# Rotary embedding and attention scores: all batch loads on SyncE's ring, and three groups of tiny loads behind stores

## The chip, the cores and the metric

The kernel runs on one core of one Trainium2 chip. The metric is the device time of that core in microseconds (us); lower is better. Engines: TensorE (PE), VectorE (DVE), ScalarE (ACT), GpSimd (POOL) and SyncE (SP), and 16 DMA engines that all queues of the core share.

## What is computed

Rotary embedding of q and k, then the scores of every query with every key, per batch and head. All is float32; batch 16, sequence 512, 16 heads of 64.

```python
q1, q2 = q[..., :half_dim], q[..., half_dim:]
q_rot = np.concatenate([q1 * cos_q - q2 * sin_q, q1 * sin_q + q2 * cos_q], axis=-1)
# k_rot from k in the same way
scores = np.einsum('bshd,bthd->bsht', q_rot, k_rot)
```

q and k are 33.6 MB each, the output is 268.4 MB.

## The kernel before, in words

The work goes in 64 steps `i`, four per batch. A step makes one output tile `st` of 128 query rows x 16 heads x 512 keys, 4 MB, and stores it with one DMA (`store`, L192). In the first batch (steps 0 to 3) the tile is stored in four quarters of 1 MB instead (L215).

Loads: q and k of a batch (2 MB each) come as one tile of 128 rows x 16 KB into `in_pool`, which has two buffers for each of q and k. Row p holds the sequence positions 4p to 4p+3. Batch 0 comes in smaller pieces (`early`) at the start. In the main loop, after step `i`, the q load of batch `i // 4 + 2` is asked for if `i % 4 == 2`, and the k load of batch `i // 4 + 3` if `i % 4 == 3`.

Compute of a step: DVE rotates the next rows of q and k (`rope`, three full-size operations each: L153, L154, L158). TensorE transposes them by a product with an identity (L174) into PSUM, from where DVE or ACT copies them into `qT` or `kT` (L189). Then `scores` makes 8 head pairs per step: two products of 64 x 128 by 64 x 512 (L205) into a PSUM tile of two banks, and one ACT copy of 128 x 1024 into `st` (L212). `stage_pool` has three buffers for `st`: ACT's first copy of step `i` has to wait until the store of step `i - 3` has landed.

What sets the order: the program is written out by hand (`tc.manual_schedule()`), so every engine issues in the order of the code. SyncE issues nearly all DMAs: the store of a step, then a load if that step asks for one, then the store of the next step. A DMA of 128 rows is cut into 8 rows for each of the 16 DMA engines. For SyncE and ACT together, the DMAs take 8 completion semaphores ("lanes") in turn, and each DMA waits for the one that had its lane before, the eighth ahead of it.

Five of the loads are made otherwise in before: those that stand in `RELIEVED` (q of batches 6, 11 and 15, k of batches 7 and 12) are made by `load_around` (L89 to L115). There GpSimd loads rows 0 to 119 as a DMA of 120 rows, which takes 15 of the DMA engines with 8 rows each. `move_cursor` issues tiny GpSimd loads into `scratch` ahead of it, which move the place at which GpSimd's next DMA starts, so that one chosen engine (`SLOW = 4`) is the one left out. The last 8 rows are loaded by a second DMA, cut into pieces of 2 KB: on ACT's queue for q, on GpSimd's for k. The issue is on POOL or ACT, so these loads do not stand in SyncE's order.

Of the kernel before, what the change touches and what calls it, by code (L numbers as in the profile page):

```python
# [10 lines left out]
def kernel(  # L11
# [8 lines left out]
    nc = tc.nc  # L20
# [53 lines left out]
    batches = {}  # L74

    RELIEVED = {("q", 6): 0, ("k", 7): 1, ("q", 11): 2, ("k", 12): 3, ("q", 15): 4}
    SLOW = 4
    scratch = const_pool.tile([P, 96], fp32, name="scratch")
    tiny = [0]  # L80

    def move_cursor(n):

        y = tiny[0]
        tiny[0] += 1
        src = bass.AP(q.tensor, 512 * y, [(512, n), (64, 2), (1, 2)])
        nc.gpsimd.dma_start(scratch[:n, 4 * y : 4 * y + 4].rearrange("p (a b) -> p a b", a=2), src)

    def load_around(which, b, t):  # L89

        n, E, SMALL = 120, C * H * D, C * H * D // 8
        x = RELIEVED[which, b]
        d = dram[which][b]

        def pieces(queue, lo, hi, F):
            k = E // F
            src = bass.AP(d.tensor, d.offset + lo * E + E - F, [(E, hi - lo), (-F, k), (1, F)])
            v = t[lo:hi].rearrange("p c e -> p (c e)")  # L100
            dst = bass.AP(v.tensor, v.offset + E - F, [v.ap[0], (-F, k), (1, F)])
            queue.dma_start(dst, src)  # L102

        if x == 0:
            nc.gpsimd.inc_swdge_sem([], [], mode="reset_dge_cursor")
        else:

            move_cursor(16 - SLOW)
        if x % 2:
            move_cursor(8)  # L110
            pieces(nc.gpsimd, n, P, SMALL)
        move_cursor(SLOW + 1)
        pieces(nc.gpsimd, 0, n, E // 2)
        if not x % 2:
            pieces(nc.scalar, n, P, SMALL)  # L115

    def load(which, b):
# [4 lines left out]
        batches[which, b] = t  # L122
        if (which, b) in RELIEVED:
            load_around(which, b, t)
# [66 lines left out]
    def store(i, st):  # L191
        nc.sync.dma_start(o_v[i // C, i % C], st)  # L192

    def scores(i, p, st):

        ps = ps_s_pool.tile([P, 2, S], fp32, tag="ps_s", name="ps")
        b = i // C
        if b == 0:
            c, hp = divmod(p, 2)
            lhs, rhs = qT[i][:, C * hp + c], kT[0][:, 2 * i + hp]  # L200
        else:
            lhs, rhs = qT[i][:, p], kT[b][:, p]
        for r in range(2):
            po, rh = ps[:, r, :], rhs[64 * r : 64 * r + 64, :]
            nc.tensor.matmul(  # L205
                out=po, lhsT=lhs[64 * r : 64 * r + 64, :], rhs=rh, start=True, stop=True
            )
        so, si = st[:, 2 * p : 2 * p + 2, :], ps
        if b > 0:
            so = so.rearrange("s r (t c) -> s r t c", c=C)  # L210
            si = si.rearrange("s r (c t) -> s r t c", c=C)
        nc.scalar.copy(out=so, in_=si)  # L212
        if b == 0 and p % 2 == 1:
            c = p // 2
            nc.sync.dma_start(o_v[0, c, :, G * i : G * (i + 1)], st[:, G * c : G * (c + 1)])  # L215
        elif b > 0 and p == HP - 1:
            store(i, st)

    def tr_act(which, n):
        for g in range(2):  # L220
            transposed(which, n, g, nc.scalar.copy)
# [5 lines left out]
    with tc.manual_schedule():  # L227
# [16 lines left out]
        for i in range(C):  # L244
            st = st_first[i] if i < 2 else stage_pool.tile([P, H, S], fp32, tag="stage", name="st")
            if i < C - 1:
                dve = rope("k", i + 1) + rope("q", i + 1) + rope("k", C + i)
                nxt = [("k", i + 1), ("q", i + 1)]
            else:
                dve = rope("q", C) + rope("k", C + i) + rope("q", C + 1) + rope("k", 2 * C)  # L250
                nxt = [("q", C), ("k", C + i)]
            for p in range(HP):
                scores(i, p, st)
                if p in (0, 1) and i > 0:
                    run(dve[:1])
                    dve = dve[1:]
                    transposed("k", C + i - 1, p, nc.vector.tensor_copy)
                if p == 3 and i < 2:
                    load("kq"[i], 2)
                if p in (2, 6):  # L260
                    m = len(dve) - (4 if p == 2 else 2) - (2 if i == C - 1 else 0)
                    run(dve[:m])
                    dve = dve[m:]
                    tr_act(*nxt.pop(0))
            run(dve)
# [3 lines left out]
        for i in range(C, NST):  # L269
            tr = {}  # L270
            if i + 1 < NST:
                tr[1], tr[3] = ("q", i + 1, 0), ("q", i + 1, 1)
            if i + C < NST:
                tr[5], tr[6] = ("k", i + C, 0), ("k", i + C, 1)
            dve = []
            if i + 2 < NST:
                dve += rope("q", i + 2)
            if i + 1 + C < NST:
                dve += rope("k", i + 1 + C)
            st = stage_pool.tile([P, H, S], fp32, tag="stage", name="st")  # L280
            for p in range(HP):
                scores(i, p, st)
                if p not in tr:
                    continue
                if tr[p][0] == "q":
                    run(dve[:1])
                    dve = dve[1:]
                    transposed(*tr[p], nc.vector.tensor_copy)
                else:
                    transposed(*tr[p], nc.scalar.copy)  # L290
            run(dve)
            if i % C == C - 2:
                load("q", i // C + 2)
            elif i % C == C - 1:
                load("k", i // C + 3)
# [30 lines left out]
```

## Time and profile before

| what | value |
|---|---|
| time, median of 2 runs | 793.2 us (792.83 to 793.57) |
| span of the profiled execution, first to last instruction | 789.9 us |
| busy: PE / ACT / DVE / POOL | 687.7 / 561.2 / 543.8 / 11.9 us |
| HBM read / written | 67.24 / 268.44 MB, 425 GB/s over the span |
| stores of 4 MB, issue to landing, median | 25.2 us |
| SyncE waiting for ACT to fill a 4 MB tile (60 stores) | 663.3 us in total |
| GpSimd's loads of 1920 KB, issue to landing, median | 29.2 us (q), 43.2 us (k) |

The span is that of one execution under the profiler; the median of the runs lies 3.3 us above it. How to read the lines that follow: "DMA" in the 40 slices is the mean busy share of the 16 DMA engines in tenths. q1 is SyncE's queue, q0 GpSimd's, q10 ACT's. In the chain of work that ended last, a line gives the start, the length and what was waited for: "DMA out_dram<-st" is the time from the issue of a store to its landing. In a timeline, the first column is the start in us from the beginning of the span, the second how long the issuing instruction (or, with xN, a run of N of them) took, and "SPq" is SyncE as the issuer.

### The profile page before, as it was taken

The page shows a single profiled execution, that of the slowest core. Times are in us where ns is not written, and L with a number is a line of the kernel's source. Part 1 is how long each engine was busy: PE and PEld are TensorE (multiplying, and loading weights), DVE is VectorE, ACT ScalarE, POOL GpSimd, SP SyncE. Part 2 cuts the span into 40 slices and gives each one's busy share as a digit, 9 for nine tenths or more (in the row PEclk, how much of TensorE's full clock was granted, in tenths as well). Part 3 has the DMA queues.
Part 4 walks back from the last instruction along what each step waited for, and adds up shares of the span by engine and source line. Part 5 has one row for each costly group of instructions (what it writes and reads, how often), then busy time and mean ns, then how long its engine had stood idle before and what let it go on. Part 6 is the DMA issues. An engine that isn't in the chain of part 4 may idle for free.

```text
span 789.9 us, 7753 instructions
## 1 busy us (share of the span) xinstructions
PE 687.7 (87%) x3072; PEld 297.4 (38%) x3072; DVE 543.8 (69%) x516; ACT 561.2 (71%) x647; POOL 11.9 (2%) x24
## 2 busy tenths in 40 slices
PE   4999998989978989798897988989899798899960
PEld 2444443433423434243343433434334343344420
DVE  7999987667855859566676666767678486587400
ACT  3888886866847868486685865877577586588770
POOL 0000000000001000000000000100000000000000
PEclk9999999999998999899899898999899899899995
DMA  9999999999999999999999999999999999999997
GB/s 353 421 426 440 429 431 435 424 434 440 428 427 429 429 425 406 428 431 436 430 431 434 427 431 427 429 432 429 427 437 422 437 433 433 428 431 436 430 431 339
DMA packets 19100, 336.18 MB, mean 426 GB/s; under 512 B 2376, under 2 KB 3656, under 8 KB 4936
## 3 DMA queue, kind: packets, MB, share of 16 engines
q1 hardware_dynamic: 16288, 324.61, 96.1%
q0 software_dynamic: 1872, 10.10, 3.1%
q10 hardware_dynamic: 904, 0.98, 0.4%
q8 instruction: 24, 0.39, 0.2%
q14 instruction: 12, 0.10, 0.0%
HBM read 67.24 MB, written 268.44 MB: 425 GB/s over the span
## 4 chain that ended last, share of the span: by engine, by line
DMA 46%; PE 39%; DVE 7%; ACT 4%; issue 1%; ACTq 0%
DMA out_dram<-st 45%; PE ps L205 29%; PE bank L174 9%; ACT st L212 4%; DVE part L153 2%; DVE early L154 1%; DVE early L158 1%; DMA early<-in_q_dram 1%; DVE k_sb L158 1%; DVE k_sb L154 1%; DVE kT_t L189 0%; DVE q_sb L154 0%; DVE q_sb L158 0%; ACTq L321 0%; DVE qT_t L189 0%
## 5 line engine op out<-in xcount | busy, mean ns | idle before, releaser
L212 ACT COPY st<-ps 128x1024 f32<-128x1024 f32 x512 | 495.0, 1020 | 193.7 <-DMA out_dram<-st 109.1
L205 PE MATMUL ps<-kT_t,qT_t 64*128 64x512 f32 x2048 | 545.6, 650 | 64.3 <-ACT st L212 64.1
L205 PEld LDWEIGHTS ps<-kT_t,qT_t 64*128 64x128 f32 x2048 | 183.3, 196 | 255.3 <-issue 135.4
L189 DVE COPY qT_t<-bank 128x512 f32<-128x512 f32 x118 | 81.5, 690 | 186.5 <-PE bank L174 186.5
L174 PEld LDWEIGHTS bank<-ident,q_sb 128*128 128x128 f32 x480 | 55.4, 151 | 100.5 <-issue 97.6
L174 PE MATMUL bank<-ident,q_sb 128*128 128x128 f32 x480 | 86.8, 308 | 0.4 <-PE ps L205 0.4
L174 PEld LDWEIGHTS bank<-ident,k_sb 128*128 128x128 f32 x480 | 50.3, 140 | 94.6 <-issue 42.3
L174 PE MATMUL bank<-ident,k_sb 128*128 128x128 f32 x480 | 78.6, 287 | 1.2 <-DVE qT_t L189 1.2
L153 DVE TENSOR_TENSOR part<-k_sb,ss_t 128x1024 f32<-128x1024 f32 x60 | 72.9, 1215 | 9.3 <-DMA k_sb<-in_k_dram 9.2
L189 ACT COPY kT_t<-bank 128x512 f32<-128x512 f32 x122 | 72.4, 598 | 6.9 <-PE bank L174 6.9
L154 DVE TENSOR_TENSOR k_sb<-k_sb,cos_t 128x1024 f32<-128x1024 f32 x60 | 73.5, 1225 | 2.0
L158 DVE TENSOR_TENSOR k_sb<-k_sb,part 128x1024 f32<-128x1024 f32 x60 | 73.5, 1225 | 2.1
L154 DVE TENSOR_TENSOR q_sb<-q_sb,cos_t 128x1024 f32<-128x1024 f32 x60 | 73.5, 1225 | 2.1
L153 DVE TENSOR_TENSOR part<-q_sb,ss_t 128x1024 f32<-128x1024 f32 x60 | 73.5, 1224 | 2.0
L158 DVE TENSOR_TENSOR q_sb<-q_sb,part 128x1024 f32<-128x1024 f32 x60 | 72.9, 1215 | 0.0
L174 PE MATMUL bank<-ident,early 128*128 128x128 f32 x64 | 10.5, 316 | 12.2 <-DVE early L158 9.7
L174 PEld LDWEIGHTS bank<-ident,early 128*128 128x128 f32 x64 | 8.3, 161 | 17.3 <-issue 13.9
L153 DVE TENSOR_TENSOR part<-early,ss_t 128x1024 f32<-128x1024 f32 x8 | 9.8, 1222 | 5.7 <-DMA early<-in_k_dram 4.9
L102 POOL DMA_DIRECT2D q_sb<-in_q_dram x3 | 2.3, 754 | 617.4 <-PE bank L174 617.4
L158 DVE TENSOR_TENSOR early<-early,part 128x512 f32<-128x512 f32 x16 | 10.3, 685 | 0.2
L154 DVE TENSOR_TENSOR early<-early,cos_t 128x1024 f32<-128x1024 f32 x8 | 9.8, 1225 | 0.3
L189 ACT COPY qT_t<-bank 128x512 f32<-128x512 f32 x10 | 5.7, 628 | 3.3 <-PE bank L174 3.3
(12 smaller groups left out, 15.9 us busy)
## 6 DMA issues: line engine op xcount, KB each, us to landing
out_dram<-st SPq DMA_DIRECT2D x60, 4096.0 KB, 25.2
k_sb<-in_k_dram SPq DMA_DIRECT2D x13, 2048.0 KB, 27.7
q_sb<-in_q_dram SPq DMA_DIRECT2D x12, 2048.0 KB, 27.6
out_dram<-st SPq DMA_DIRECT2D x16, 1024.0 KB, 14.5
q_sb<-in_q_dram POOLq DMA_DIRECT2D x3, 1920.0 KB, 29.2
k_sb<-in_k_dram POOLq DMA_DIRECT2D x2, 1920.0 KB, 43.2
early<-in_k_dram SPq DMA_DIRECT2D x1, 1536.0 KB
early<-in_q_dram SPq DMA_DIRECT2D x1, 1536.0 KB, 12.4
```

Source lines behind the costliest of these rows:

```text
L102: queue.dma_start(dst, src)
L153: nc.vector.tensor_tensor(pv, xs, ss, op=mult)
L154: nc.vector.tensor_tensor(xc, xc, cs, op=mult)
L158: nc.vector.tensor_tensor(y, y, z, op=add)
L174: nc.tensor.transpose(bank[:, x, :], src, ident)
L189: copy(out=dst, in_=src)
L205: nc.tensor.matmul(out=po, lhsT=lhs[64 * r : 64 * r + 64, :], rhs=rh, start=True, stop=True)
L212: nc.scalar.copy(out=so, in_=si)
```

## The change

`RELIEVED` is emptied, so `load_around` and `move_cursor` are called no more and all 30 batch loads after batch 0 are made by SyncE (L126 before, L132 after). A new function `marks` issues 15 tiny loads on SyncE, of n = 1 to 15 rows of three float32 each, into columns of `scratch` that nothing reads. It is called right behind the store of steps 10, 34 and 60, so ahead of the q load that steps 10 and 34 ask for.

```diff
-    RELIEVED = {("q", 6): 0, ("k", 7): 1, ("q", 11): 2, ("k", 12): 3, ("q", 15): 4}
+    RELIEVED = {}
...
+    def marks():
+
+        for n in range(1, 16):
+            src = bass.AP(q.tensor, 512 * n, [(4096, n), (1, 3)])
+            nc.sync.dma_start(scratch[:n, 45 + 3 * n : 48 + 3 * n], src)
...
         elif b > 0 and p == HP - 1:
             store(i, st)
+            if i in (10, 34, 60):
+                marks()
```

In the compiled order this takes 19 rows from POOL and six from ACT's list, and adds 50 to SyncE's: 45 tiny loads and the 5 batch loads. The orders of TensorE and DVE stay as they were.

## Prediction

> **What bounds the kernel now.** I read the page first, then the chain that ended last, then SyncE's issues, then the trace's records of single packets and landings. From the page:
>
> ```profile
> span 789.9 us, 7753 instructions
> ...
> DMA  9999999999999999999999999999999999999997
> GB/s 353 421 426 440 429 431 435 424 434 440 428 427 429 429 425 406 428 431 436 430 431 434 427 431 427 429 432 429 427 437 422 437 433 433 428 431 436 430 431 339
> ...
> q1 hardware_dynamic: 16288, 324.61, 96.1%
> q0 software_dynamic: 1872, 10.10, 3.1%
> ```
>
> The 16 DMA engines are busy from the first slice to the last; the two queues alone make 99.2%. No engine of the core stands at that share all along. So the end is set by the slowest of the 16 engines, and what counts is how much that one has to do and how long it stands idle. The chain's longest pieces show its pace:
>
> ```profile
> 113.28 25.54 DMA out_dram<-st
> 159.42 28.77 DMA out_dram<-st
> 207.39 30.89 DMA out_dram<-st
> 260.35 24.02 DMA out_dram<-st
> 305.15 30.61 DMA out_dram<-st
> 356.54 28.25 DMA out_dram<-st
> 406.99 27.18 DMA out_dram<-st
> 455.57 28.16 DMA out_dram<-st
> 505.95 23.87 DMA out_dram<-st
> 550.84 29.48 DMA out_dram<-st
> 599.51 29.51 DMA out_dram<-st
> 649.81 29.32 DMA out_dram<-st
> 739.70 20.22 DMA out_dram<-st
> ```
>
> Start plus length is when a store has landed in full, on its last engine: steps 8, 12, 16, ... 52, then 60. Landings are 138.82, 188.19, 238.28, 284.37, 335.76, 384.79, 434.17, 483.73, 529.82, 580.32, 629.02, 679.13, 759.92. Four steps move four stores and two loads, 20.97 MB. In the packet records a 32 KB packet takes 1.21 us on every engine, a store so 9.7 us, a load 4.85, and four steps would be 48.5. The differences are 49.37, 50.09, **46.09**, 51.39, 49.03, 49.38, 49.56, **46.09**, 50.50, 48.70, 50.11. The two short ones are where GpSimd issued two loads each around one engine (from 227.75 and 472.79). All others are longer than 48.5: one engine is late. The packet records name no engine, but each packet starts 3 to 4 ns before the end of the one ahead of it, so chains can be followed: on one engine packets take 10 to 50 ns over the 1213, some 1 us in every 50 and 15.5 us in all; the other fifteen have exactly 1213, but for some lumps.
>
> The last thing to see is what SyncE does behind store 10, which it issued at 133.44 (the last of the x3):
>
> ```profile
> 113.28 20.50 SPq L192 DMA_DIRECT2D out_dram<-st  x3
> 133.87 0.56 SPq L126 DMA_DIRECT2D q_sb<-in_q_dram  x1
> 149.40 0.33 SPq L192 DMA_DIRECT2D out_dram<-st  x1
> ```
>
> By its landing events store 10 lands between 154.98 (first engine) and 158.64 (last). The load behind it and store 11 stand in the rings long before: that is why the engines never run dry.
>
> **Part 1: the loads go back to SyncE's ring.** Removed: on POOL 5 big loads, 2 of 8 rows and 11 tiny ones, on ACT 3 loads of 8 rows. POOL does nothing else, and ACT gets back under 3 us of issue (3 x 0.7 to 1.3) while it waits for DMA anyway (109.1 us of idle before the copies of L212): no gain. SyncE issues 5 loads more, 5 x 0.5 us, in stretches in which it waits for ACT (663.3 us in its waits): no cost. The bytes are the same. What goes is the relief. I extend the chain without it. Seven of the unrelieved differences (all but the two right after a relief, 51.39 and 50.50, in which all engines had long packets) have a mean of 49.46. Eleven of these from 138.82 end at 682.9, against 679.13. Steps 53 to 60 hold 8 stores and one load, 82.45 us, at that pace 84.1: 767.0, against 759.92. The three last stores and the rest took 30.0, at that pace 30.6: 797.6. So the relief's loss is **+7.7 us**. Ends: with 49.03, the difference farthest from any POOL load, the same sum gives +2.0; with the mean of all nine unrelieved, 49.79, it gives +12.0. I take 7.7, since another count comes near it: an engine with no drip and no extra rows would end near 780.5, plus 15.5 of drip is 796.
>
> **Part 2: the marks.** In the compiled order every DMA of SyncE waits for the semaphore lane of the DMA eight places ahead of it; there are 8 lanes. Before, that one had always landed. Now 15 marks stand behind store 10 (and 34, and 60). Marks 1 to 7 wait for older transfers and at latest for store 9; mark 8 has the lane of the store itself and waits for it **to land**. SyncE issues in order, so marks 9 to 15, the load of q (steps 10 and 34) and the next store, long filled, are all held behind mark 8. When the store's last engine ends, nothing is left in any ring. From then on, per group:
> - last packet to landing to wake: 0.4 us (the last packet of the kernel ends 788.62, landed 789.02);
> - marks 8 to 15 issued, 8 x 0.49 us. Small loads at the start are the nearest rows:
>
> ```profile
> 0.74 0.43 SPq L70 DMA_DIRECT2D early<-in_k_dram  x1
> 1.23 0.45 SPq L230 DMA_DIRECT2D cos_t<-in_cos_dram  x1
> ```
>
>   0.74 to 1.23, and the next one at 1.74: 0.49 and 0.51 apart, so 3.9 us. Marks 9 to 15 wait for marks 1 to 7, which sit right behind the store and land with it. The next big DMA waits for mark 8 too, but a small first load landed 2.9 us after its issue (sin_t), which is within the 3.9;
> - its issue to its first packet: 1.1 us (0.74 to the first data packet at 1.82).
>
> Sum 5.4 us in which the late engine is idle, and the others longer. Nothing covers it: no other ring holds work now. It is not won back, since the engines are the bound. PE and ACT do not prolong it: they fill the other two stage buffers meanwhile, so that two stores follow at once. Three groups: **+16.2 us**. The transferred bytes (1.4 KB a group) are nothing. Ends: a spacing of 0.43 (133.44 to 133.87) gives 4.9 a group, and 4.6 with a faster start, 13.8 in all; the spacing of ACT's loads of 8 rows, 0.73 at least and 0.78 with a gap, gives 7.7, 23 in all. Nearest are SyncE's own small loads, so 5.4.
>
> **Sum.** Span 789.9 + 7.7 + 16.2 = 813.8. The two runs' median, 793.2, lies 3.3 above the profiled span; with that, **817 us**.
>
> **Rivals.**
> *The late engine is late because of GpSimd's loads.* For it: in the stretches around 244 to 287, 491 to 532 and 688 to 692 its packets take 1.4 to 1.6 us in place of 1.21, some 11 us in all, a cost of the relief itself that goes with it. If the small drip went too, four steps would take 48.5: the same sum gives 784.8, so -5.1, and with the marks 789.9 - 5.1 + 16.2 + 3.3 = **804**, not slower by 2%. Against it: between 138.82 and 188.19, before the first big POOL load, the pace is 49.37 already. It decides if four steps take under 48.86 us. [...]
> *The marks cost nothing.* If mark 8 did not wait for its own store, 15 x 0.49 = 7.4 us of issue would fit between 133.87 and 149.40, where SyncE idles: 789.9 + 7.7 + 3.3 = **801**, no change. For it: SyncE's lanes never showed as a wait before. Against it: the compiled order names the store's own lane at mark 8, in all three groups.
> *The marks cost more*, 7.7 a group, with the relief at +12: 789.9 + 12 + 23 + 3.3 = **828**.
>
> **How the numbers follow.** 2% of 793.2 is 15.9 us, about what a measurement of this kernel can tell from no change: slower is above 809.1, faster below 777.3. My forecast, with its own bounds 809 (2.0 and 13.8) to 828, has 0.78, the dear end included. The late engine cured has 0.12, free marks 0.08, something not seen that makes it faster 0.02. Slower 0.78, within 2% 0.20, faster 0.02. The range for 8 in 10 takes in the cured engine and leaves out the free marks: 804 to 828; the forecast's own is 809 to 828.
>
> **What would show it.** SyncE's waits have a new row, a mark waiting for DMA out_dram, three times up to some 25 us. The line of DMA shares dips at about 158, 463 and 778 us, for 5 to 6 us each on the late engine. The chain's four-step differences lose their 46.09s and stay near 49.5. No POOL load is left, and no packets of 1.5 us. I am wrong on part 1 if unstopped stretches take 48.5 for four steps, and on part 2 if the load of q behind store 10 is issued before that store lands, or starts in under 4 us or over 8 after it.

## The result, and the profile after

The changed kernel takes **817.69 us** (two runs, 817.62 and 817.77) against 793.2 before: ratio 1.0306, 95% interval 1.0276 to 1.0336. The forecast was 817. The profiled span is 815.8 us, 25.9 more than before.

The page of the changed kernel, the lines that answer to those of before:

```profile
span 815.8 us, 7760 instructions
...
DMA  9999999699999999999999599999999999999958
GB/s 346 421 424 438 430 428 432 279 378 440 433 421 427 435 435 426 437 428 433 432 427 439 215 411 434 431 432 427 434 428 426 441 434 427 430 435 430 428 245 386
...
q1 hardware_dynamic: 17728, 335.10, 96.4%
```

GpSimd's queue is gone, and the row of DMA shares has three holes, at slices 8, 23 and 39, where a group of marks stands. SyncE's waits say what made them (us in total, times, longest):

```profile
SPq L198 <- ACT st L218: 607.7, 58, 23.7
SPq L93 <- DMA out_dram<-st: 55.1, 7, 9.7
SPq L221 <- ACT st L218: 48.1, 15, 13.6
```

The second line is new: marks that wait for a store to land. It is seven waits of up to 9.7 us: in the first group marks 6, 7 and 8 wait one after another for the stores of steps 8, 9 and 10, in the two others marks 7 and 8 for the last two stores. The trace names the same semaphore for such a pair: 103, 104 and 105 for stores 8, 9 and 10, and for marks 6, 7 and 8 behind them. The timeline of SyncE around step 10:

```profile
134.09 28.36 SPq L93 DMA_DIRECT2D scratch<-in_q_dram  x15
162.97 0.36 SPq L132 DMA_DIRECT2D q_sb<-in_q_dram  x1
163.44 0.37 SPq L198 DMA_DIRECT2D out_dram<-st  x1
163.93 0.35 SPq L132 DMA_DIRECT2D k_sb<-in_k_dram  x1
164.37 28.96 SPq L198 DMA_DIRECT2D out_dram<-st  x3
```

The load of q is issued at 162.97, which was 133.87 before, and three more DMAs follow within 2 us: all were ready and stood behind the marks. By the landing events store 10 landed at 159.5, mark 8 was issued at 159.48, and mark 15 at 162.06. The stretches around it (us; then busy time of PE, PEld, DVE, ACT, POOL; granted clock, DMA share, GB/s):

```profile
150.00:155.00 5.00, 5.00 (x26) 2.10 (x22) 2.97 (x3) 4.33 (x6) 0.00 (x0) 1.00 0.99 426
155.00:159.00 4.00, 4.00 (x22) 1.80 (x20) 3.78 (x4) 3.33 (x5) 0.00 (x0) 1.00 0.28 115
159.00:164.00 5.00, 5.00 (x27) 2.21 (x25) 4.28 (x5) 4.34 (x6) 0.00 (x0) 1.00 0.07 15
164.00:171.00 7.00, 7.00 (x36) 3.13 (x34) 4.76 (x5) 6.19 (x8) 0.00 (x0) 1.00 1.07 358
171.00:176.00 5.00, 2.70 (x14) 0.91 (x10) 3.86 (x4) 0.40 (x1) 0.00 (x0) 1.00 0.98 419
```

From 155 to 159 the fast DMA engines have already run dry (28% busy) and wait for the slowest; from 159 to 164 nothing but marks moves; PE works on through both. From 164 to 171 the engines are fully "busy" (a packet counts whole in the stretch in which it starts, so the share can pass 1) but move 358 GB/s, not 430: of the 128 packets of the load of q, the first transfer after the hole, 54 take 0.73 to 2.1 us in place of 0.61. That was not foreseen. In the packet records the time without any big packet (16 KB or more) is 4.99, 4.59 and 4.44 us in the three groups, 14.0 in all, and the two slow loads take another 1.7 us per engine each.

### The profile page after: what moved, and what is told of

It is laid out like the page before. It is cut to its first block, busy times and chain, and to the rows that moved or that the text cites. A ratio compares the mean times of both kernels' runs of the same rounds, so it can differ in the third digit from the quotient of the medians.

```text
span 815.8 us, 7760 instructions
## 1 busy us (share of the span) xinstructions
PE 684.3 (84%) x3072; PEld 296.4 (36%) x3072; DVE 544.2 (67%) x516; ACT 561.0 (69%) x647; POOL 0.7 (0%) x6
## 4 chain that ended last, share of the span: by engine, by line
DMA 49%; PE 36%; DVE 6%; ACT 4%; issue 1%; SPq 0%; ACTq 0%; DVEq 0%
DMA out_dram<-st 47%; PE ps L211 28%; PE bank L180 9%; ACT st L218 4%; DMA k_sb<-in_k_dram 2%; DVE part L159 2%; DVE k_sb L164 1%; DVE k_sb L160 1%; DVE early L164 1%; DVE early L160 1%; DVE kT_t L195 0%; DVE q_sb L160 0%; DVE q_sb L164 0%; SPq L70 0%; ACTq L329 0%
## 5 line engine op out<-in xcount | busy, mean ns | idle before, releaser
L164 DVE TENSOR_TENSOR early<-early,part 128x512 f32<-128x512 f32 x16 | 10.3, 686 | 0.2
L195 DVE COPY kT_t<-bank 128x512 f32<-128x512 f32 x6 | 4.1, 683 | 0.0
```

The lines of the kernel that those rows point to most:

```text
L164: nc.vector.tensor_tensor(y, y, z, op=add)
L195: copy(out=dst, in_=src)
```

## The experiments

Two theories stood at the start. **A**, the forecast's: one DMA engine is late by itself, the relief was worth 7.7 us, and the marks cost because each group drains all rings. **B**: the engine was late because of GpSimd's loads, and the marks cost all of the loss. **C** rivals A on the marks: each costs by its own issue or packets, not by a wait. Differences below are taken against the kernel before on the same chip (792.56 us in the first four runs, 793.08 in the last four).

### Each half of the change alone

Without relief and without marks:

```diff
-            if i in (10, 34, 60):
-                marks()
```

> The first part of the change alone: RELIEVED is empty, marks are not called. Theory A (the late DMA engine is late by itself, and the relief is worth 7.7 us): 801 us, four steps of the chain near 49.5 us all along, SyncE never waiting for a store's landing. Rival B (the engine is late because of GpSimd's loads, and the marks cost all of the 24.5 us): 788 to 794 us.

Measured: **800.16 us**, 7.6 more than before, ratio 1.0096 (1.0081 to 1.0111). The longest pieces of its chain:

```profile
112.68 25.79 DMA out_dram<-st
160.57 27.33 DMA out_dram<-st
209.18 28.69 DMA out_dram<-st
257.06 30.26 DMA out_dram<-st
308.10 28.67 DMA out_dram<-st
358.70 27.52 DMA out_dram<-st
407.00 28.69 DMA out_dram<-st
457.66 27.46 DMA out_dram<-st
505.90 28.66 DMA out_dram<-st
556.59 27.40 DMA out_dram<-st
605.20 28.25 DMA out_dram<-st
655.52 27.87 DMA out_dram<-st
```

Landings (start plus length) are 138.47, 187.90, 237.87, 287.32, 336.77, 386.22, ... 683.39. Nine of the eleven differences are 49.43 to 49.47 us: the late engine's own pace, the 49.46 of the forecast, with no GpSimd load in the program. Its drip in the packet records (what packets take over their usual time, where that is under 0.1 us each) is 17.8 us. How late it is in the end shows in the last stretches:

```profile
780.00:788.00 8.00, 0.00 (x0) 0.00 (x0) 0.00 (x0) 0.00 (x0) 0.00 (x0) 0.54 0.95 410
788.00:797.00 9.00, 0.00 (x0) 0.00 (x0) 0.00 (x0) 0.00 (x0) 0.00 (x0) 0.50 0.08 33
```

In the last 9 us the DMA share is 0.08, about one engine of 16: by the landing events the last store is done on 12 of 16 engines at 788.4 to 788.6 and on the late one at 797.5. Theory B is out.

With the relief and with the marks:

```diff
-    RELIEVED = {}
+    RELIEVED = {("q", 6): 0, ("k", 7): 1, ("q", 11): 2, ("k", 12): 3, ("q", 15): 4}
```

> The second part alone: the kernel before, with the marks behind the stores of steps 10, 34 and 60. Theory A (each group drains the rings; after the drain the load of q is slow too, so 18 us in all by the profile of the change): 809 to 812 us, that is the two parts add up. Rival B: 817 us, the whole loss.

Measured: **818.14 us**, ratio 1.0318 (1.0303 to 1.0334). Theory A's sum missed by 6 to 9 us, and the number is rival B's, though B had just fallen: beside the marks the relief is worth nothing. The stretches around step 10 are those of the change (from 159 to 164 us a DMA share of 0.08), so the marks did not get dearer there. But the store of step 60 still lands at 781.8, as without relief (781.4). In the change the late engine was the last by 2.4 us there (781.4, the next 779.0); with relief others were (781.8 and 781.7). That GpSimd's loads had held these up is likely, not shown. This asked for a theory of its own, **E**: a drain holds every engine until the latest has ended. So the time is the sum over the stretches of the latest engine in each, and what an engine gains in one stretch does not pay for another. The landings agree: from store 10 to store 34 the change takes 303.6 us and the kernel with relief 304.7, from 34 to 60 it is 318.3 and 317.7. A run further down tests it.

### What in the marks costs

Only marks of 1 to 6 rows, so that none has the store's lane:

```diff
-        for n in range(1, 16):
+        for n in range(1, 7):
```

> The change with marks of 1 to 6 rows only. Theory A (what costs is mark 8, which has the store's own lane): now no mark has it; the next load waits for the store before, and the store after the next DMA has the lane, so the rings still hold one transfer when it is released: about 801 us, as without marks. Rival C (every mark costs by itself, by its issue or its small packets): 6/15 of the marks' 16 to 18 us stays, so 807 to 808 us.

Measured: **802.61 us** (801.09 to 803.56), ratio 1.0131 (1.0114 to 1.0147): 2.4 more than without marks by the median, 0.8 by the profiled span (799.3). Of the 17.5 us that 15 marks cost, at most a seventh is left with six of them. SyncE's waits:

```profile
SPq L198 <- DMA out_dram<-st: 32.3, 4, 9.6
SPq L329 <- DMA out_dram<-st: 20.2, 1, 20.2
SPq L132 <- DMA out_dram<-st: 18.6, 2, 9.6
```

SyncE waits for landings here too, 50.9 us in the first and the third line (the second is the kernel's end), and it hardly costs anything: the wait ends while the rings still hold a transfer (DMA share 0.99, 1.05 and 0.98 in the three stretches of 5 us from 155 to 170). So it is neither the marks' number nor SyncE's waiting, but the empty rings.

Marks of 1 to 8 rows, so that the one with the store's lane is the last:

```diff
-        for n in range(1, 16):
+        for n in range(1, 9):
```

> The change with marks of 1 to 8 rows: the one that waits for the store is kept, the seven behind it are gone. Theory A (idle time per group = landing and wake 0.4, one mark issued 0.4, SyncE's next issue and first packet 1.5, so 2.3 in place of 4.9, and the slow load of 1.9 behind it in two groups): 801 + 3 x 2.3 + 2 x 1.9 = 812 us. Rival C (price by number of marks): 8/15 of 17, so 810 us; told apart by the length of the gap in the profile, 2.3 us against 4.9.

Measured: **809.03 us**, ratio 1.0204 (1.0189 to 1.022). Both theories named a time near it (812 and 810); the gap decides. From its timeline:

```profile
133.49 24.99 SPq L93 DMA_DIRECT2D scratch<-in_q_dram  x8
158.59 0.36 SPq L132 DMA_DIRECT2D q_sb<-in_q_dram  x1
159.05 0.37 SPq L198 DMA_DIRECT2D out_dram<-st  x1
```

The load follows its last mark (issued at 158.21) at 158.59. The time without big packets is 1.89, 1.88 and 1.75 us, nearer to A's 2.3 than to the 4.9 of C. Gaps of 5.5 us plus the two slow loads (3.1 here) are 8.6; measured against the kernel without marks, 8.9. The seven marks behind the wait cost (14.0 - 5.5) / 21 = 0.40 us each: behind the wait their number counts, ahead of it hardly.

The marks of steps 10 and 34 behind the load of q, so that a store comes first after the drain:

```diff
-            store(i, st)
-            if i in (10, 34, 60):
-                marks()
...
                 load("q", i // C + 2)
             elif i % C == C - 1:
                 load("k", i // C + 3)
+            if i in (10, 34, 60):
+                marks()
```

> The change, with the 15 marks of steps 10 and 34 issued behind the load of q in place of ahead of it; at step 60, which has no load, nothing moves. Mark 8 then waits for that load, and the first transfer after the drain is a store. Theory A (the groups at steps 10 and 34 cost 4.9 us of idle and 1.9 us more because the load that comes first after the drain runs with long packets; a store behind a drain, as at step 60, does not): 817.7 - 3.8 = 814 us. Rival (any first transfer is slow, or the 1.9 us is no loss): 817 to 818 us.

Measured: **816.5 us** (815.61 to 816.69), ratio 1.0294 (1.0278 to 1.0309). Between the two, and undecided by the time. The trace says why: the store behind the hole is slow only at its very end (packets of 1.6 to 2.3 us from 176.4), and the load of k behind that store is slow too (issued at 167.46, it ends 6.0 us after the store on most engines, where 4.85 is usual). The sum of long packets around the hole is the same, some 30 us over 16 engines. So what is slow is not "the first transfer" but the first load after a drain. The second one is not: in the change the load of k behind the first hole is 0.15 us per engine over its usual time, the load of q ahead of it 1.75.

### What makes the late engine late, and what the relief is

Another engine left out, in the kernel before:

```diff
-    SLOW = 4
+    SLOW = 12
```

> The kernel before with SLOW = 12 in place of 4: the same loads by GpSimd, around another DMA engine. Theory A (one engine is late by itself and it is the one that before leaves out; the long packets of 1.4 to 1.6 us during GpSimd's loads are on that engine too): the 800.2 us without relief and up to 11 more, 805 to 811 us. If the long packets are on the engine left out, whichever it is: 800 us. Rival (leaving out any engine helps, or GpSimd's issue itself): 793 us.

Measured: **803.33 us** (802.47 to 806.03), ratio 1.0137 (1.0115 to 1.0159), 10.3 more than before and some 3 more than without relief; why more, and not the same, was not settled. That leaving out any engine helps is out. Nor did the late engine lose the 5 to 11 us by which theory A would have put GpSimd's long packets on it: at step 24 it lands at 338.9, against 336.8 without relief. The long packets (16.6 us in the stretches of the POOL loads; 1.1 in the same stretches without relief) go with the engine left out, whichever it is. The records name no engine, but on one engine each big packet starts only 3 to 4 ns before the end of the one ahead of it, so the late engine's small excesses and long packets of its own cannot run side by side. In before, long packets in close order fill 38 us, and only 8 packets that are 10 to 60 ns over fall into these, 2 in 10 us where the whole run has 5: there the long ones are the late engine's, which is the one left out. With the other engine left out, 42 fall into 48 us: the two kinds run side by side, on two engines. So the long packets eat a part of what the relief takes off: one engine, presumably the one left out and two loads or 9.7 us lighter after the first pair, lands only 2.3 us ahead of the next at step 22 (300.2 against 302.5).

Relief, and marks at step 60 alone, as a test of theory E:

```diff
-            if i in (10, 34, 60):
+            if i == 60:
```

> The kernel before with the marks at step 60 alone. Relief and all marks together took 818.1, no less than the marks without relief (817.7). Theory E (a drain lets no engine go ahead of the latest, so the time is the sum of the latest engine of each stretch, and relief in one stretch does not pay for another; with one drain near the end the relief keeps its worth): 792.6 + 4.4 to 5.4 = 797 to 798 us. Rival F (relief and marks hinder each other wherever they stand): 800.2 + 4.4 to 5.4 = 805 us.

Measured: **797.56 us**, ratio 1.0059 (1.0042 to 1.0076): theory E's number. Relief beside one late drain keeps its worth, relief between drains loses it.

Each matmul as two halves, without relief or marks:

```diff
-            po, rh = ps[:, r, :], rhs[64 * r : 64 * r + 64, :]
...
+            for y in range(2):
+                po = ps[:, r, 256 * y : 256 * y + 256]
+                rh = rhs[64 * r : 64 * r + 64, 256 * y : 256 * y + 256]
...
```

> Neither relief nor marks, and each matmul of 512 columns made as two of 256, so 4096 PE and weight-load instructions more and the same transfers. Asks what makes the late engine late. Theory G (something that goes with every instruction that is executed takes a little of this DMA engine): its drip, 17.8 us in the profile of the kernel without relief and marks, grows with the instructions from 7.7 to 11.8 thousand to about 27 us, and the time from 800 to 808 or 810 us. Rival (its drip has nothing to do with instructions): 800 us, as PE needs 10 us of the 12.3 us of a step.

Measured: **808.25 us** (807.66 to 809.0), ratio 1.0192 (1.0177 to 1.0208), 15.2 above before where the kernel without relief is 7.6 above. Of its page:

```profile
span 805.9 us, 11811 instructions
...
q8 instruction: 40, 0.66, 0.3%
```

and of its chain:

```profile
210.61 29.18 DMA out_dram<-st
259.50 30.31 DMA out_dram<-st
312.27 27.45 DMA out_dram<-st
361.02 28.60 DMA out_dram<-st
411.67 27.85 DMA out_dram<-st
```

The four differences of these landings (239.79, 289.81, 339.72, 389.62, 439.52) are 50.02, 49.91, 49.90 and 49.90, where it was 49.45 with 4,096 instructions fewer. The drip in the packet records grows from 17.8 to 29.8 us. At the end the late engine lands at 804.9, the others at 795.2 to 796.0. PE is no nearer to being the bound: it is busy for 699.0 us (87%), 686.9 (86%) without the halves. So the bytes are the same, no POOL load is there, and the drip is 67% larger with 53% more instructions; in the nine other kernels, all with 7.7 to 7.8 thousand, it is 15.5 to 21.0 us. What slows the late engine grew with the executed instructions. Which work that is stays open. The queue that the page calls "instruction" (q8) has 40 packets in place of 24, 16 more that take 15 us together, but they are not on the late engine: followed from packet to packet, the engine that has one of them shows at most 2 packets with a small excess in the 10 us to either side, where the late engine shows 5 to 16 (54 of these packets, between 90 and 750 us of the two runs).

## Why the prediction was right, step by step

The landings of the changed kernel's chain answer to those of before:

```profile
113.10 26.86 DMA out_dram<-st
164.37 32.99 DMA out_dram<-st
219.13 27.49 DMA out_dram<-st
267.39 28.02 DMA out_dram<-st
317.64 26.60 DMA out_dram<-st
365.95 27.72 DMA out_dram<-st
414.45 28.66 DMA out_dram<-st
467.56 32.96 DMA out_dram<-st
522.59 27.37 DMA out_dram<-st
```

They land at 139.96, 197.36, 246.62, 295.41, 344.24, 393.67, 443.11, 500.52 and 549.96. The differences are **57.40**, 49.26, 48.79, 48.83, 49.43, 49.44, **57.41** and 49.44. Those of 46.09 are gone, as forecast. The two with a group of marks are 8.3 us longer than the mean of the nine others up to step 52 (49.14), more than the 5.4 of the forecast; some 4.8 of it is the hole and 1.7 the slow load. The others are a little shorter than the 49.45 without marks, which gives the rest back: from store 10 to store 34 it is 303.6 us against 297.2 without marks, 6.4 more.

- **Part 1, the relief: +7.7 forecast, +7.6 measured** (800.16 against 792.56, alone). The pace it was built on, 49.46, was met with 49.43 to 49.47. The rival of the cured engine fell: without any GpSimd load the drip is 16.7 us with the marks and 17.8 without. The marks themselves show which engine it is. A mark of n rows has n landings, those of the mark before and one more. At step 60 those of 1 to 4 rows landed at 774.7 to 776.0; those of 5 to 7 rows have one landing at 781.6 to 782.0, just behind the store's last at 781.4. So it is the fifth engine in this order, and the one that `SLOW = 4` leaves out: with relief and marks, the mark of 5 rows is down at 780.0 there, ahead of the store's last at 781.8.
- **No price on POOL, ACT and for SyncE's issues**: right. The pace alone gave a span of 797.6 us without the marks, and 798.5 was measured.
- **Packets of 1.5 us gone**: right as a sign. What they take over their 1.21 us, in the stretches of the POOL loads, was 15.7 us in before and is 0.8 now. That they sat on the late engine was read rightly, since before leaves that engine out; but they come with being left out, as the run with another engine left out shows, and are no sign of what makes the engine late.
- **Part 2, the marks: +16.2 forecast, +17.5 measured** (817.69 against 800.16). The mechanism was right: mark 8 is issued when its store has landed, and the load of q 3.5 us later. Two sizes were off and partly cancel, which is luck. Marks follow each other in 0.31 to 0.41 us, not in 0.49, so the idle time is 14.0 us and not 16.2. And the loads behind two of the holes are slow, 3.4 us that the sum had nothing for; 17.4 together.
- **The step from span to time: 3.3 us forecast, 1.9 measured** (817.69 against a span of 815.8). The span was forecast as 813.8 and missed by 2.0. So the sum comes within 0.7 us of the time partly by luck.
- **"Three times up to some 25 us"**: wrong in form. It is seven waits of up to 9.7 us, since mark 7, and once mark 6, wait for the stores before the last one; it changes no time.
- **Free marks** fell by that wait, and by the run with eight marks. The dear end was not needed.
- **That the two parts add** was taken for granted and holds in one order only. Without relief, marks cost 17.5. With it they cost 25.6 (818.14 less 792.56), and the relief is worth nothing. By theory E a drain ends the account of each stretch. One drain at step 60 with the relief costs 4.5 us and not 25.6, which is what E, and not a sum, gives for these two.

The best version stays the kernel before: none of the nine others has a median below 797.

## What to carry to other kernels

In this kernel, where the 16 DMA engines are the bound, what counted of a new DMA was not its bytes (1.4 KB in a group of 15) but what it waited for. In a kernel like it, look in the compiled order for a new DMA's completion semaphore's last user, and see whether that is the transfer just ahead on the same ring: here all that stood behind such a mark started from empty rings, after 4.4 to 5.0 us without a big packet in the groups of 15. Six marks in a group cost 0.8 to 2.4 us, eight 8.9 and fifteen 17.5, so the price hung on the one that waits for the transfer just ahead, and on what still had to be issued behind it. Evening out the engines' load paid here only between two points at which all of them meet: 7.6 us with no drain, nothing with three (818.14 with the relief, 817.69 without). Price such edits by stretch, on the latest engine in each.

## What the runs showed of the hardware

- One of the 16 DMA engines, the fifth in the order of the marks' rows, is late with no GpSimd load in the program, by some 2 us in every 100, and more with more instructions: a drip of 17.8 us over the span with 7,715 of them (15.5 to 21.0 in all kernels with that many or a few more), 29.8 with 11,811. The packets of the queue "instruction" are not on this engine (54 followed); the cause was not settled.
- GpSimd's loads of 120 rows leave one engine out: in the packet records of before, followed from packet to packet from 474 to 502 us and from 668 to 700, one engine has none of a load's 240 packets of 8 KB, the others 14 to 18 each. It is also the late one, with 11 and 12 small excesses in these stretches, the others at most one each. Which engine is left out goes with the rows of the tiny loads that `SLOW` sets: 793.08 us with `SLOW = 4`, 803.33 with 12.
- The engine left out runs with packets of 1.4 to 1.6 us in place of 1.21 while they last, by the count of small excesses beside them (8 in 38 us and 42 in 48). The five loads, some 22 us lighter on it (an estimate: 5 x 4.85, less 8 packets of 2 KB and 0.08 us that it has of the last 8 rows of each of the three loads of q), gain only 7.6 us. How much of the difference is these packets is not shown: in before five engines land the last store within 0.8 us of each other (788.3 to 789.0), so the others bound the gain as well.
- The first load after a drain is slow: 49 to 54 of its 128 packets take 0.73 to 2.1 us in place of 0.61, some 1.7 us per engine and drain in the change, and it is slow with a store between drain and load too. The load after it is not. Why was not tried.
- A tiny load on empty rings landed 1.3 us after its issue (mark 8, 159.48 to 160.74), where a load of 64 KB at the kernel's start took 2.9 in before.
